# Order of VectorE, GpSimd and ScalarE work around the seven-product gate and up matmuls of a two-block transformer kernel

## The chip, the cores and the metric

One core of a Trainium2 chip runs the whole program. The metric is the device time of one execution in microseconds (us). TensorE is PE in the profile (its weight loads PEld), VectorE is DVE, ScalarE is ACT, GpSimd is POOL, and SyncE (SP) issues the DMAs.

## What is computed

Two blocks of two layers each work on 512 tokens of width 1024. Every one of the four layers ends in a gated feed-forward part with 2816 hidden columns, and the change lies in that part alone:

```python
def rms_norm(x, g):
    xf = x.astype(jnp.float32)
    y = xf * lax.rsqrt(jnp.mean(xf * xf, axis=-1, keepdims=True) + EPS)
    return (y * g.astype(jnp.float32)).astype(x.dtype)

# first block, both layers
    h = rms_norm(x, g_ffn_pre)
    gate, up = jnp.split(jnp.matmul(h, w_gate_up), [FFN_HIDDEN], axis=-1)
    f = jnp.matmul(jax.nn.silu(gate) * up, w_down)
    return x + rms_norm(f, g_ffn_post)

# second block, both layers
def swiglu(xn, w_gate, w_up, w_down):
    return (jax.nn.silu(xn @ w_gate) * (xn @ w_up)) @ w_down
        h = h + swiglu(rmsnorm(h, norm_ffn[l]), ffn_w_gate[l], ffn_w_up[l], ffn_w_down[l])
```

Ahead of it stand retention, dilated attention and a spatial gate (first block), or sparse attention or a convolution and cross attention (second block). They are as they were.

## The kernel before

All values are float32. A product of two float32 matrices is made of three TensorE passes (`mm3`, L384 to L387): each operand is held as a high half (ScalarE casts it to the rounded type, "cast") and a low half (VectorE subtracts the high half from the source, "low"), and high times high, high times low and low times high are summed in a PSUM bank.

`ffn` (L565) is called once for each of the four layers. The normalised input lies turned in `xh` and `xl` (8 blocks of 128 x 512 tokens). The four token blocks reach it one after the other: `settle` (L436) adds a block's result into `x`, `sq` squares it on ScalarE (L425), `sc` scales it on VectorE (L430), `transposer` (L401) turns it on TensorE (L407), casts it (L395) and takes the low part (L396). In the first block (`post` is true) `settle` also scales the two PSUM banks on VectorE (L457) and adds them (L461). The first two hidden blocks of 128 (`prod`, L580) are computed as plain products, for tokens 0 to 255 first, while blocks 2 and 3 of the tokens still arrive.

The other 20 hidden blocks go in 20 **units**: a unit is a pair of weight tiles, gate for two hidden blocks (even units) or up for the same two (odd units). `seven` (L666) computes a unit's 2 x 2 product of halves with seven half-size products instead of eight, 12 matmuls of 256 columns each. For that a unit's weights are prepared on the way: `unit` (L257) has the steps `cast1`/`low1` (tile a, slot s1), `t13` (two GpSimd subtractions in place of tile b and a, L283 and L284; the first overwrites a's first half, so it must come after `low1`), `cast4`/`low4` (half of b), `t24` (two VectorE subtractions, L287 and L288, which need `t13` and `low4` done), `cast2`/`low2` and `cast3`/`low3`. The low parts are all L270, the casts L266. On the other side the products are combined: ScalarE copies the first (L700, `m1`), VectorE adds (L705, L714, L718, L723, L724), the last sum of a unit is `whole_sum` (L684), followed for gate units by the silu on ScalarE (L686), and after an up unit `gated` multiplies up into gate (L690).

The order is written by hand: after product r of unit i the function s_r of unit i queues its share of both kinds of work (L694 to L726), so that VectorE's queue holds, unit after unit, L287, L288, L718, low2, L723, L724, low3, L684, low1, (L690 after an up unit,) L705, low4, L714. The products' sums of the input (`act` s1 to s4) are made once, from four whole copies of input quarters: two by `whole` (L629) on GpSimd, two copied by ScalarE out of the transposes' banks (L417), combined on VectorE (`mix`, L633) and split (L640, L644).

PSUM has eight banks b0 to b7. In `seven` the third product takes bank 2 in even units and bank 7 in odd ones. The down product (`down`) follows, in all eight banks: block t of the tokens takes banks 2t and 2t+1. Its weights are split by `pump` (casts L249, lows L250), its inputs by `hsplit` (cast L395, low L396 into `sh`). `_Clock` (L165) only orders the recording; the engines run by semaphores.

Of the kernel before, what the change touches and what calls it, by code (L numbers as in the profile page):

```python
# [199 lines left out]
class _Weights:  # L200
# [53 lines left out]
            if not moved:  # L254
                return

    def unit(self):  # L257

        V, S, G = self.nc.vector, self.nc.scalar, self.nc.gpsimd
        u = {}  # L260
# [19 lines left out]
        def t13():  # L280
            b = u["b"] = self.r.pop(u["j"])
            u["b12"], u["b22"] = (b[:, 512 * i:512 * i + 512] for i in range(2))
            G.tensor_sub(u["b11"], u["b12"], u["b11"])  # L283
            G.tensor_sub(u["b12"], u["b12"], u["b22"])  # L284

        def t24():
            V.tensor_sub(u["b22"], u["b22"], u["b11"])  # L287
# [35 lines left out]
def tile_mixers(ctx: ExitStack, tc: tile.TileContext, a: dict, widths: list, out: bass.AP):  # L323
# [48 lines left out]
    def bank(i):  # L372
        return psum.tile([P, T], F32, tag=f"b{i}", name=f"b{i}")
# [25 lines left out]
    def transposer(xn, t, dst, banks):  # L399
        dh, dl = dst  # L400

        def go(halves=(0, 1)):
            for half in halves:
                b = bank(banks[half])
                for kk in range(4):
                    k = 4 * half + kk
                    PE.transpose(b[:, kk * P:(kk + 1) * P], xn[:, k * P:(k + 1) * P], ident)  # L407
                ks = slice(4 * half, 4 * half + 4)
                if dl is None:
                    S.copy(dh[:, ks, cols(t)], blocks(b))  # L410
                else:
                    split_from(dh[:, ks, cols(t)], dl[:, ks, cols(t)], blocks(b))
                    if keep["x"] is not None and dh is xh and t > 1:
                        kept.append((keep["x"][half][:, :, (t - 2) * P:(t - 1) * P], blocks(b)))
                        keep["t"].add(t)
            while kept:
                S.copy(*kept.pop(0))  # L417
        return go

    turned = {}  # L420
# [144 lines left out]
    def ffn(pend, post, nxt, last=False):  # L565
# [82 lines left out]

        def unit(i):
            if i not in ops:  # L650
                ops[i] = W.unit()
            return ops[i]

        def prep(i, *names):
# [13 lines left out]
        def seven(i):  # L668


            n, j = units[i]
            b1, b2, b3, b6, b7, b45 = (bank(k) for k in (0, 1, 2 + 5 * (i % 2), 3, 4, 5 + i % 2))
            p1, p2, p3, p6, p7 = (z[:, :256] for z in (b1, b2, b3, b6, b7))
            p4, p5 = b45[:, :256], b45[:, 256:]
            m1, u2, u3, u4 = (st["pc"][:, 256 * k:256 * k + 256] for k in range(4))
# [16 lines left out]
            last = done[-2] if i else (lambda: None,) * 2  # L692

            def s0():  # L694
                last[0]()
                W.done(int(i > 0))
                prep(i + 1, "low1")

            def s1():
                S.copy(m1, p1)  # L700
                prep(i + 1, "t13")
                last[1]()

            def s2():
# [24 lines left out]
            for r, (p, f) in enumerate(zip(todo, (s0, s1, s2, s3, s4, s5, s6))):  # L729
                product(i, *p)  # L730
                f()
                if i == 0 and r == 0:
                    sum_low("s1", 3)()
                if i == len(units) - 1:
                    if r == 5:
                        hsplit(0)
                    W.pump(1)
                W.prefetch()
                yield

# [12 lines left out]
        late = len(steps) - 4  # L753
        keep.update(x=(quarter(full(0)), quarter(full(3))), t=set())

        def fill(t):
            if t not in keep["t"] and turned[t]:
                for half in range(2):
# [3 lines left out]

        def unit0(*names):
            return lambda: prep(0, *names)
        also(0, whole(1, 0, 0, G), unit0("cast1"))
        also(1, whole(2, 4, 0, G), unit0("low1"))
        also(2, lambda: fill(2))
        also(late - 1, lambda: fill(2), lambda: fill(3), lambda: keep.update(x=None), unit0("t13", "cast4"), mix(3, 0, 3, 1), mix(4, 3, 1, 0), mix(2, 2, 4, 0),
             sum_high("s2", 4), sum_high("s4", 2))
        also(late, unit0("low4"), sum_low("s4", 2), unit0("t24", "cast2"), sum_low("s2", 4))  # L770
        also(late + 1, unit0("low2"), mix(0, 0, 1, 0), sum_high("s3", 0))
# [8 lines left out]
            g = seven(i)  # L780
            steps += [(12 * 0.119, lambda g=g: next(g))] * 7
        steps.append((0, last_sums))
        steps.append((0, lambda: (two(0), nxt(), hsplit(1))))

        TAIL = 4
        acc = {}
# [1197 lines left out]
```

## Time and profile before

| | |
|---|---|
| median of 3 runs | 2797.47 us (2794.26 to 2797.48) |
| the profiled execution | 2799.59 us, of which the profiled span is 2797.8 us |
| PE busy | 2677.8 us, 96% of the span, 16568 matmuls |
| DVE busy | 1809.4 us, 65% |
| ACT busy | 1182.2 us, 42% |
| POOL busy | 782.4 us, 28% |
| chain that ended last, by engine | PE 51%, DVE 23%, POOL 12%, ACT 10%, issue 4% |

The first four engine rows are busy time; a busy PE is not a PE at its peak, since matmuls are pipelined. The last row follows the work that ended last backwards from the final instruction, each step to what released it. Rows further down have the start in us from the span's start, the duration in us, engine, line, operation, written and read tiles with shapes, and in brackets the engine's idle time before the instruction and what ended it.

### The profile page before, as it was taken

What the parts mean: (1) busy time and instruction counts of PE and PEld (TensorE: products, weight loads), DVE (VectorE), ACT (ScalarE), POOL (GpSimd) and SP (SyncE); (2) the same over time, 40 slices, a digit from 0 to 9 for tenths busy, and PEclk for the clock granted to TensorE, in tenths of its full rate; (3) what the DMA queues carried; (4) which work ended last, traced back from release to release, by engine and by line L of the source; (5) the groups of instructions that cost most, each with busy time, mean ns of one, the idle gap of its engine ahead of it and who ended that gap; (6) DMA issues with size and microseconds to landing.
All of it is one profiled execution on the core that took longest, in us unless ns stands there. A gap on an engine that the chain in (4) does not pass through costs nothing.

```text
span 2797.8 us, 41468 instructions
## 1 busy us (share of the span) xinstructions
PE 2677.8 (96%) x16568; PEld 2378.7 (85%) x16568; DVE 1809.4 (65%) x2733; ACT 1182.2 (42%) x2015; POOL 782.4 (28%) x662
## 2 busy tenths in 40 slices
PE   8999999999999999999999999999998889999999
PEld 7888999889788999878677889998886578899987
DVE  4555888545565888453985437887379744488852
ACT  3434444333434444333444434444256544344431
POOL 3231333002232232012451312331049913133300
PEclk9999999999999999999999999999999999999999
DMA  4221232323121323423232212333232312133331
GB/s 154 78 68 67 91 106 98 130 75 108 61 80 53 102 98 101 138 70 102 64 124 83 91 38 91 106 103 124 91 119 91 113 30 92 46 91 106 99 116 65
DMA packets 76225, 256.42 MB, mean 92 GB/s; under 512 B 10368, under 2 KB 11776, under 8 KB 76032
## 3 DMA queue, kind: packets, MB, share of 16 engines
q1 hardware_dynamic: 76032, 253.77, 28.3%
q8 instruction: 130, 2.13, 0.3%
q14 instruction: 63, 0.52, 0.1%
HBM read 251.64 MB, written 2.10 MB: 91 GB/s over the span
## 4 chain that ended last, share of the span: by engine, by line
PE 51%; DVE 23%; POOL 12%; ACT 10%; issue 4%; DMA 1%; POOLq 0%; ACTq 0%; DVEq 0%; SPq 0%
PE b L385 15%; PE b L387 15%; PE b L386 14%; DVE hl L270 8%; ACT hl L266 5%; POOL raw L283 5%; POOL raw L284 4%; DVE raw L287 2%; DVE hl L250 2%; DVE b L1759 2%; DVE hraw L684 2%; ACT hl L249 1%; PE b L407 1%; PE b L1639 1%; DVE xn L430 1%
## 5 line engine op out<-in xcount | busy, mean ns | idle before, releaser
L385 PE MATMUL b<-xh,hl 128*128 128x256 f32 (+1 forms) x1728 | 505.5, 293 | 4.0 <-DVE xn L457 2.4
L386 PE MATMUL b<-xl,hl 128*128 128x256 f32 (+1 forms) x1728 | 504.1, 292 | 1.7 <-DVE xl L396 1.7
L387 PE MATMUL b<-xh,hl 128*128 128x256 f32 (+1 forms) x1728 | 503.6, 291 | 0.0
L266 ACT CAST hl<-raw 128x1024 fp32r<-128x1024 f32 x320 | 286.7, 941 | 391.1 <-DVE raw L287 391.1
L385 PE MATMUL b<-hl,xh 128*128 128x512 f32 (+2 forms) x1152 | 439.1, 381 | 4.9 <-ACT xh L395 3.1
L386 PE MATMUL b<-hl,xh 128*128 128x512 f32 (+2 forms) x1152 | 422.6, 367 | 1.7 <-DVE hl L250 1.7
L387 PE MATMUL b<-hl,xl 128*128 128x512 f32 (+2 forms) x1152 | 423.0, 367 | 0.2
L270 DVE TENSOR_TENSOR hl<-raw,hl 128x1024 fp32r<-128x1024 f32 x320 | 387.1, 1210 | 9.4 <-ACT hl L266 1.3
L250 DVE TENSOR_TENSOR hl<-raw,hl 128x1024 fp32r<-128x1024 f32 (+2 forms) x249 | 303.4, 1232 | 137.8 <-ACT hl L249 135.7
L249 ACT CAST hl<-raw 128x1024 fp32r<-128x1024 f32 (+2 forms) x308 | 303.5, 1000 | 101.9 <-PE b L387 60.1
L385 PEld LDWEIGHTS b<-xh,hl 128*128 128x128 f32 x1728 | 331.4, 192 | 11.4 <-issue 3.4
L386 PEld LDWEIGHTS b<-xl,hl 128*128 128x128 f32 x1728 | 331.3, 192 | 7.8 <-DVE xl L396 2.7
L387 PEld LDWEIGHTS b<-xh,hl 128*128 128x128 f32 x1728 | 331.2, 192 | 5.4
L283 POOL TENSOR_TENSOR raw<-raw 128x512 f32<-128x512 f32 x80 | 140.2, 1752 | 567.3 <-DVE hl L270 502.7
L387 PE MATMUL b<-hl,sh 128*128 128x512 f32 x704 | 276.3, 392 | 7.2 <-DVE sh L396 7.2
L385 PE MATMUL b<-hl,sh 128*128 128x512 f32 x704 | 276.7, 393 | 2.2 <-ACT sh L395 2.2
L387 PE MATMUL b<-sh,hl 128*128 128x256 f32 x960 | 270.8, 282 | 5.8 <-DVE hl L270 5.8
L386 PE MATMUL b<-hl,sh 128*128 128x512 f32 x704 | 276.0, 392 | 0.0
L385 PE MATMUL b<-sh,hl 128*128 128x256 f32 x960 | 269.2, 280 | 1.1 <-ACT hraw L576 1.1
L386 PE MATMUL b<-sh,hl 128*128 128x256 f32 x960 | 267.9, 279 | 0.0
L385 PEld LDWEIGHTS b<-hl,xh 128*128 128x128 f32 x1152 | 219.3, 190 | 35.1 <-issue 7.0
L386 PEld LDWEIGHTS b<-hl,xh 128*128 128x128 f32 x1152 | 219.4, 190 | 25.9 <-DVE hl L250 3.0
(304 smaller groups left out, 4745.2 us busy)
## 6 DMA issues: line engine op xcount, KB each, us to landing
raw<-in_ws SPq DMA_DIRECT2D x400, 512.0 KB, 3.6
raw<-in_ws SPq DMA_DIRECT2D x64, 384.0 KB, 3.1
x<-in_x SPq DMA_DIRECT2D x4, 512.0 KB, 6.6
mem<-in_mem SPq DMA_DIRECT2D x4, 512.0 KB, 5.6
out<-x SPq DMA_DIRECT2D x4, 512.0 KB, 2.6
raw<-in_ws SPq DMA_DIRECT2D x4, 336.0 KB, 2.8
gain<-in_g_mix_pre SPq DMA_DIRECT2D x2, 512.0 KB, 4.7
gain<-in_g_mix_post SPq DMA_DIRECT2D x2, 512.0 KB, 4.4
```

Source lines behind the costliest of these rows:

```text
L249: self.nc.scalar.copy(t[:, 0, :w], r[:, :w])
L250: self.low.tensor_sub(t[:, 1, :w], r[:, :w], t[:, 0, :w].bitcast(F32))
L266: S.copy(u[name][:, 0, :n], src())
L270: return lambda: V.tensor_sub(u[name][:, 1, :n], src(), u[name][:, 0, :n].bitcast(F32))
L283: G.tensor_sub(u["b11"], u["b12"], u["b11"])
L284: G.tensor_sub(u["b12"], u["b12"], u["b22"])
L287: V.tensor_sub(u["b22"], u["b22"], u["b11"])
L385: PE.matmul(o, lh, rh, start=first, stop=False)
L386: PE.matmul(o, lh, rl, start=False, stop=False)
L387: PE.matmul(o, ll, rh, start=False, stop=last)
L684: V.tensor_add(c[:, :, 256:], u3[:, None, :].to_broadcast([P, 2, 256]), halves(b45))
L1759: V.scalar_tensor_tensor(acc[g], i, w, acc[g], op0=OP.mult, op1=OP.add)
```

## The change

Five things change, all in `ffn` and what it calls.

- In a unit's first step, the next unit's `low1` and `t13` are queued ahead of the finished unit's `whole_sum`; they stood behind it.
- For the first unit of each `ffn` the two subtractions of `t13`, and for each `ffn` the two `whole` sums, run on VectorE instead of GpSimd.
- ScalarE's copies of turned input (`kept`) are no longer queued right behind their transposes but by `flush`, two steps of the plan later, behind casts of weights.
- The third product's bank is swapped: 7 in even units, 2 in odd ones.
- In the last unit, weight tiles of the down product are split after four of the seven products instead of all, and the first two hidden blocks are split after products 4 and 5 (the first was after product 5, the second behind the last sum).

```diff
-    def unit(self):
+    def unit(self, first=False):
...
-            G.tensor_sub(u["b11"], u["b12"], u["b11"])
-            G.tensor_sub(u["b12"], u["b12"], u["b22"])
+            e = V if first else G
+            e.tensor_sub(u["b11"], u["b12"], u["b11"])
+            e.tensor_sub(u["b12"], u["b12"], u["b22"])
...
-            while kept:
-                S.copy(*kept.pop(0))
...
-                ops[i] = W.unit()
+                ops[i] = W.unit(not i)
...
-            b1, b2, b3, b6, b7, b45 = (bank(k) for k in (0, 1, 2 + 5 * (i % 2), 3, 4, 5 + i % 2))
+            b1, b2, b3, b6, b7, b45 = (bank(k) for k in (0, 1, 7 - 5 * (i % 2), 3, 4, 5 + i % 2))
...
             def s0():
+                prep(i + 1, "low1", "t13")
                 last[0]()
                 W.done(int(i > 0))
-                prep(i + 1, "low1")
 
             def s1():
                 S.copy(m1, p1)
-                prep(i + 1, "t13")
                 last[1]()
...
                 if i == len(units) - 1:
-                    if r == 5:
-                        hsplit(0)
-                    W.pump(1)
+                    if r in (0, 2, 4, 6):
+                        W.pump(1)
+                    if r in (4, 5):
+                        hsplit(r - 4)
...
+        def flush():
+            while kept:
+                S.copy(*kept.pop(0))
...
-        also(0, whole(1, 0, 0, G), unit0("cast1"))
-        also(1, whole(2, 4, 0, G), unit0("low1"))
-        also(2, lambda: fill(2))
-        also(late - 1, lambda: fill(2), lambda: fill(3), ...
+        us, g = steps[0]
+        steps[0] = (us, lambda g=g: (whole(1, 0, 0, V)(), g()))
+        also(0, whole(2, 4, 0, V), unit0("cast1"))
+        also(1, unit0("low1"))
+        also(2, flush, lambda: fill(2))
+        also(late - 1, flush, lambda: fill(2), lambda: fill(3), ...
...
-        steps.append((0, lambda: (two(0), nxt(), hsplit(1))))
+        steps.append((0, lambda: (two(0), nxt())))
```

What it moves in VectorE's queue, at three places. Lines of the kernel after are one to three off those before (L683 is `whole_sum`, L689 `gated`, L703 was L705, L712 was L714, L288 was L287). First, in the middle of the units of the first layer, around an up unit's last sum (b_2993). Before:

```order
L270 TENSOR_TENSOR hl<-raw,hl 128x1024
L684 TENSOR_TENSOR hraw<-pc,b_2993 128x2x256
L270 TENSOR_TENSOR hl<-raw,hl 128x1024
L690 TENSOR_TENSOR hraw<-hraw 128x1024
L705 TENSOR_TENSOR hraw<-pc,b_3107 128x256
L270 TENSOR_TENSOR hl<-raw,hl 128x512
```

After:

```order
L270 TENSOR_TENSOR hl<-raw,hl 128x1024 x2
L683 TENSOR_TENSOR hraw<-pc,b_2993 128x2x256
L689 TENSOR_TENSOR hraw<-hraw 128x1024
L703 TENSOR_TENSOR hraw<-pc,b_3107 128x256
L270 TENSOR_TENSOR hl<-raw,hl 128x512
```

`low1` (the second L270) now stands directly behind `low3` and ahead of the sum and of `gated`. Second, VectorE at the start of the first layer's `ffn`, from the transposes of token block 2 (banks b_2337, b_2344) to those of block 3 (b_2474, b_2481). Before:

```order
L396 TENSOR_TENSOR xl<-b_2344,xh 128x4x128
L250 TENSOR_TENSOR hl<-raw,hl 128x1024
L457 SCALAR_TENSOR_TENSOR xn<-b_2253,sm,gain 128x512
L457 SCALAR_TENSOR_TENSOR xn<-b_2254,sm,gain 128x512
L461 TENSOR_TENSOR x<-x,xn 128x1024
...
L396 TENSOR_TENSOR xl<-b_2481,xh 128x4x128
L633 TENSOR_TENSOR hraw<-hraw 128x1024 x3
```

After:

```order
L397 TENSOR_TENSOR xl<-b_2344,xh 128x4x128
L628 TENSOR_TENSOR hraw<-xh,xl 128x1024
L250 TENSOR_TENSOR hl<-raw,hl 128x1024
L628 TENSOR_TENSOR hraw<-xh,xl 128x1024
L456 SCALAR_TENSOR_TENSOR xn<-b_2253,sm,gain 128x512
...
L397 TENSOR_TENSOR xl<-b_2481,xh 128x4x128
L284 TENSOR_TENSOR raw<-raw 128x512
L285 TENSOR_TENSOR raw<-raw 128x512
L632 TENSOR_TENSOR hraw<-hraw 128x1024 x3
```

The two `whole` sums (L628) and the first unit's `t13` (L284, L285) are new in this queue. Third, VectorE in the last unit of the first layer, where L705, L714 and L724 read banks 1, 3 and 7. Before:

```order
L250 TENSOR_TENSOR hl_4909<-raw_4752,hl_4909 128x1024
L705 TENSOR_TENSOR up_4876<-pc_2628,b1_4871 128x256
L714 TENSOR_TENSOR pc_2628<-pc_2628,b3_4873 128x256
L718 TENSOR_TENSOR pc_2628<-pc_2628,b4_4874 128x256
L396 TENSOR_TENSOR sh_4965<-hraw_2336,sh_4965 128x512
L723 TENSOR_TENSOR pc_2628<-pc_2628,b6_4875 128x256
L724 TENSOR_TENSOR up_4876<-pc_2628,b7_4872 128x256
L684 TENSOR_TENSOR up_4876<-pc_2628,b6_4875 128x2x256
L690 TENSOR_TENSOR hraw_2336<-hraw_2336,up_4876 128x1024
L396 TENSOR_TENSOR sh_4988<-hraw_2336,sh_4988 128x512
```

After:

```order
L703 TENSOR_TENSOR up_4876<-pc_2628,b1_4871 128x256
L250 TENSOR_TENSOR hl_4922<-raw_4752,hl_4922 128x1024
L712 TENSOR_TENSOR pc_2628<-pc_2628,b3_4873 128x256
L397 TENSOR_TENSOR sh_4952<-hraw_2336,sh_4952 128x512
L716 TENSOR_TENSOR pc_2628<-pc_2628,b4_4874 128x256
L397 TENSOR_TENSOR sh_4968<-hraw_2336,sh_4968 128x512
L721 TENSOR_TENSOR pc_2628<-pc_2628,b6_4875 128x256
L722 TENSOR_TENSOR up_4876<-pc_2628,b2_4872 128x256
L683 TENSOR_TENSOR up_4876<-pc_2628,b6_4875 128x2x256
```

The splits of the first two hidden blocks (`sh`) stand earlier, and L722 reads bank 2 where L724 read bank 7. ScalarE's queue here has the same kinds of instructions in the same order as before; the orders of TensorE and of the DMAs have not moved.

## Rows read from the trace of the kernel before

**Rows 1.** Waits of PE, whole run: waiter, releaser, us in total, times, longest.

```profile
PE b L387 <- DVE hl L270: 5.8, 24, 0.3
PE b L385 <- DVE xn L457: 2.4, 2, 1.2
PE b L387 <- DVE sh L396: 7.2, 4, 1.8
```

**Rows 2.** Waits of PE from 268 to 502 us, the first layer's gate and up.

```profile
PE b L407 <- DVE xn L430: 0.9, 2, 0.5
```

**Rows 3.** Timeline of PE: third product of two even units, one pair apart.

```profile
331.19 0.28 PE L385 MATMUL b<-sh,hl 128*128 128x256 f32 x1
...
351.21 0.28 PE L385 MATMUL b<-sh,hl 128*128 128x256 f32 x1
```

**Rows 4.** Timeline of DVE over two units, first layer.

```profile
472.27 0.69 DVE L287 TENSOR_TENSOR raw<-raw 128x512 f32<-128x512 f32 x1 [0.86 <-POOL raw L284]
...
477.15 0.68 DVE L684 TENSOR_TENSOR hraw<-pc,b 128x512 f32<-128x512 f32 x1
477.74 1.22 DVE L270 TENSOR_TENSOR hl<-raw,hl 128x1024 fp32r<-128x1024 f32 x1
479.21 0.42 DVE L705 TENSOR_TENSOR hraw<-pc,b 128x256 f32<-128x256 f32 x1 [0.25 <-ACT pc L700]
479.73 1.15 DVE L270 TENSOR_TENSOR hl<-raw,hl 128x512 fp32r<-128x512 f32 x1
...
482.07 0.69 DVE L287 TENSOR_TENSOR raw<-raw 128x512 f32<-128x512 f32 x1 [0.85 <-POOL raw L284]
...
487.54 1.22 DVE L270 TENSOR_TENSOR hl<-raw,hl 128x1024 fp32r<-128x1024 f32 x1
488.68 1.22 DVE L690 TENSOR_TENSOR hraw<-hraw 128x1024 f32<-128x1024 f32 x1
490.03 0.42 DVE L705 TENSOR_TENSOR hraw<-pc,b 128x256 f32<-128x256 f32 x1
490.37 1.23 DVE L270 TENSOR_TENSOR hl<-raw,hl 128x512 fp32r<-128x512 f32 x1
...
492.78 0.69 DVE L287 TENSOR_TENSOR raw<-raw 128x512 f32<-128x512 f32 x1 [0.86 <-POOL raw L284]
```

**Rows 5.** Timeline of POOL over the same two units.

```profile
479.04 1.30 POOL L283 TENSOR_TENSOR raw<-raw 128x512 f32<-128x512 f32 x1 [6.80 <-DVE hl L270]
...
488.84 2.21 POOL L283 TENSOR_TENSOR raw<-raw 128x512 f32<-128x512 f32 x1 [6.81 <-DVE hl L270]
491.12 1.62 POOL L284 TENSOR_TENSOR raw<-raw 128x512 f32<-128x512 f32 x1
```

**Rows 6.** Timeline of ACT behind a gate unit's last sum.

```profile
477.86 1.06 ACT L686 ACTIVATE hraw<-hraw 128x1024 f32<-128x1024 f32 x1 [1.92 <-DVE hraw L684]
478.82 0.35 ACT L700 COPY pc<-b 128x256 f32<-128x256 f32 x1
```

**Rows 7.** Timeline of DVE at the start of the first layer's gate and up.

```profile
281.72 2.31 DVE L430 SCALAR_TENSOR_TENSOR xn<-x,sm,gain 128x1024 f32<-128x1024 f32 x1 [0.77 <-POOL sm L392]
...
287.45 1.23 DVE L633 TENSOR_TENSOR hraw<-hraw 128x1024 f32<-128x1024 f32 x1 [0.65 <-ACT hraw L417]
```

**Rows 8.** Timeline of POOL at the same place.

```profile
281.65 1.30 POOL L283 TENSOR_TENSOR raw<-raw 128x512 f32<-128x512 f32 x1
283.02 2.13 POOL L284 TENSOR_TENSOR raw<-raw 128x512 f32<-128x512 f32 x1
```

**Rows 9.** Timeline of DVE at the start of the first layer's down product.

```profile
503.95 0.68 DVE L396 TENSOR_TENSOR sh<-hraw,sh 128x512 fp32r<-128x512 f32 x1
...
505.00 0.42 DVE L724 TENSOR_TENSOR up<-pc,b 128x256 f32<-128x256 f32 x1
```

**Rows 10.** Timeline of PE at the same place.

```profile
504.69 0.50 PE L387 MATMUL b<-hl,sh 128*128 128x512 f32 x1 [1.80 <-DVE sh L396]
```

**Rows 11.** Busy times by stretch, PEclk (share of 2.4 GHz) third from the end.

```profile
505.25:508.60 3.35, 3.35 (x9) 2.59 (x8) 3.31 (x6) 2.31 (x4) 0.00 (x0) 0.51 0.71 251
```

More of the change, by code (lines that the diff above doesn't have):

```diff
@@ L764, in unit0 @@
             return lambda: prep(0, *names)
-        also(0, whole(1, 0, 0, G), unit0("cast1"))
-        also(1, whole(2, 4, 0, G), unit0("low1"))
-        also(2, lambda: fill(2))
-        also(late - 1, lambda: fill(2), lambda: fill(3), lambda: keep.update(x=None), unit0("t13", "cast4"), mix(3, 0, 3, 1), mix(4, 3, 1, 0), mix(2, 2, 4, 0),
+        us, g = steps[0]
[3 more added lines that the diff above has]
+        also(2, flush, lambda: fill(2))
+        also(late - 1, flush, lambda: fill(2), lambda: fill(3), lambda: keep.update(x=None), unit0("t13", "cast4"), mix(3, 0, 3, 1), mix(4, 3, 1, 0), mix(2, 2, 4, 0),
              sum_high("s2", 4), sum_high("s4", 2))
```

## The prediction
> **What bounds the kernel now.** TensorE is busy 96% of the span, so only its waits can be won. I read in this order: what PE waits for, PE's own pace where it doesn't wait, and then the queues of the engines it waits for.
>
> PE's waits that end in the lines touched here are four kinds [rows 1, 2]: 24 waits for a low part (L270), 7.2 us for the first split hidden block at the start of the four down products (L396), 2 x 1.2 us for L457, and 0.9 us for L430. They look small, but what they stand for is larger. Where PE doesn't wait, the third product of two even units lies 351.21 - 331.19 = 20.02 us apart [rows 3], 168 matmuls of 0.119 us. VectorE's queue needs 492.78 - 472.27 = 20.51 us for the same two units [rows 4], and stands waiting for GpSimd's L284 before L287 in both, 0.86 and 0.85 us. So VectorE and GpSimd are slower than PE by 0.49 us in each pair of units. PE starts the stage some way ahead of them in what it has ready: of nine pairs in a layer only the last six show a wait (24 in four layers), so the reserve is about 9 x 0.49 - 6 x 0.49 = 1.5 us. At the end of a stage it is gone, and **the end of each gate and up stage is set by the VectorE chain, not by PE**. That chain runs low1, then GpSimd's t13 (L283, L284), then L287, L288, low2, low3, L684 and low1 again.
>
> How the two engines meet is in the same rows. L283 takes 1.30 us when it comes first (479.04), and low4, 128 x 512 elements, then takes 1.15 instead of L287's 0.69: it ends 0.54 us after L283 does. Behind L690, which started at 488.68 and ends at 489.90, L283 takes 2.21 and ends 1.15 us after L690 [rows 4, 5]. L705, whose second input lies in PSUM, takes its 0.42 us beside L283 and neither is lengthened. So instructions with both inputs in SBUF exclude each other on the two engines, for their whole length, whoever comes first. At the stage's start it goes the other way round: L283 at 281.65 first, L430 held to 2.31 us, and L284 held to 2.13 behind L430, although L430 had been waiting when L283 ended [rows 7, 8].
>
> The Trainium skill, "SBUF — State Buffer", section "Who interferes with whom", states this as a rule: a VectorE instruction with two SBUF inputs and a GpSimd instruction that reads SBUF take one shared interface, and the one issued first blocks the other fully. The trace agrees. It speaks against the change in one place: low1 earlier lets L283 go ahead of L690, so L690 is now the one that is blocked. By the rule an up unit comes to the 10.55 us worked out below, without it to some 9.7, which is the first rival.
>
> **The units.** Nothing is added; low1 moves ahead of L684, and t13 behind low1 with it. I lay out both units from the start of L287 (0).
>
> Behind a gate unit (L287 at 472.27) L684 starts now at 4.88 and low1 ends at 6.69. After: low1 4.88 to 6.10, L684 6.02 to 6.70. GpSimd starts 0.08 behind low1: L283 6.18 to 7.48, L284 7.56 to 8.85, if nothing holds it. But the silu (L686) waits for L684, ScalarE's copy L700 stands behind the silu, and L705 waits for the copy [rows 4, 6]: silu 6.73, copy 7.69 to 8.04, L705 8.07, low4 0.52 later at 8.59. There it is held by L284 to 8.85 and ends 0.54 later, 9.39; L714 0.4 more, next L287 at 9.70. Before it was 9.80 (482.07). So of the 0.60 us by which low1 is earlier only 0.1 is left: low1 used to fill the time of the silu, and now VectorE idles there 1.4 us.
>
> Behind an up unit (L287 at 482.07): low1 ends at 6.10, L283 6.18 to 7.48. L690 wants to start at 6.74, is held to 7.48 and needs 1.07 more: 8.55. L284, held by L690, ends 1.13 later at 9.68. L705 0.13 behind L690, 8.68; low4 is held to 9.68, ends 10.22; L714 from 10.14, L287 at 10.55. Before it was 10.71. The port's pieces are the same (L283, L690, L284, low4), only in another order, so 0.16 is won and not 0.60.
>
> A pair becomes 9.70 + 10.55 = **20.25 us instead of 20.51**, still above PE's 20.02. Nine pairs: 9 x 0.26 = 2.3 us a layer earlier at the end of the chain. PE's waits fall from 2.9 us to 9 x 0.23 - 1.5 = 0.6 a layer.
>
> **The start.** The `whole` sums on VectorE are two more instructions of 1.22 us (the size of L690) in front of L457, but the low part that stood there held by GpSimd's sums no longer is; and t13 on GpSimd no longer holds L430 (1.2 instead of 2.31). I take the 1.2 us for L457 and 0.5 for L430 as won in the two layers of the first block: 1.7 us. In the second block there is no L457, and L430 isn't waited for. Against it, the first unit's t13 now costs VectorE 2 x 0.69 = 1.38 us ahead of L633; 0.65 of it falls into a wait that L633 has now for ScalarE's copies [rows 7], 0.7 stays on the chain. Together -1.0 in each of two layers, +0.7 in each of the other two: **-0.6 in all**. Bounds: if the 0.65 doesn't cover, +1.3 more in four layers; if the 0.7 meets the reserve, -2.8. The bank swap takes away one PE wait at the third product of the first unit (0.3 us), but the chain then lags PE there and takes it back: nothing. The copies behind the casts: ScalarE has nothing waiting at that place, nothing.
>
> **The end.** In the last unit the order of casts stays; on VectorE the first split L396 comes ahead of L718 and behind only one L250 that had to wait, by my addition 0.6 us earlier than at 503.95 + 0.68 now [rows 9]. But L724 now reads bank 2, which the down product wants six matmuls after its first, and the second split stands ahead of it: L724 would end at about 505.76 instead of 505.42. PE, which waits for the split until 504.69 [rows 10], reaches that bank four matmuls later (4 x 0.24), at 505.73; after, 505.82 at equal lag. So +0.1 a layer, **+0.4 in all**; the 0.6 is paid back at the bank.
>
> **The clock.** In the first layer the granted clock is 0.51 just after this gap [rows 11], the 1.2 GHz level, for 3.35 us, at a cost of about 3.35 x 0.49 = 1.6 us; the same follows in three of the four layers. PE's idle time there becomes shorter and is cut in three pieces (0.7, 1.2 and 0.7 us instead of 0.7 and 1.8). Whether the clock still falls no row tells: from none (-5) to all four (+1.6). I take two, **-1.6**.
>
> **Sum.** 4 x -2.3 = -9.2, -0.6, +0.4, -1.6: -11.0 us. The profiled execution took 2799.59, 2.1 above the median; the same difference from the median of 2797.47 gives **2786.5 us**.
>
> **Rivals.**
> *PE's own pace.* If L690 isn't held behind L283 (the rows show low4 and L430 held, L690 never in second place), its unit takes some 9.7 too, the pair drops under 20.02, and PE bounds the stage. Chain: 9 x 0.49 = 4.4 a layer, PE's waits gone, clock never falling: 4 x -4.4 - 0.6 + 0.4 - 5 = -23, 2774.5. The ending of low4 after L283 speaks against it. Chance 0.14.
> *Little changes.* The up unit's gain of 0.16 comes from a difference of order alone, and the gate unit's 0.10 from a ScalarE chain whose gaps I took from another order. If both vanish, the pair stays at 20.4 to 20.5: 4 x -0.5 - 0.2, and the clock as now: 2795. The split of the wait would then only have moved from L287 to L690 and L705. Chance 0.18.
> *Slower.* When L283 ends, L690 and L284 both want the port. If L284, 0.08 us behind, gets it, L690 ends 1.3 us later: L284 7.56 to 8.85, L690 to 9.92, L705 10.05, low4 10.4 to 11.1, L287 at 11.4. Pair 21.1, 9 x 0.6 = 5.4 a layer: 4 x 5.4 - 0.2 = +21, 2819. It turns to a loss when the pair passes 20.52. L430 at 281.72, which went ahead of L284, is the evidence against. Chance 0.08.
> My forecast has the other 0.60, with 2781 to 2791 of its own (0.1 us a pair is 3.6 us; one fall of the clock 1.6).
>
> **Numbers.** Within 0.2% (5.6 us, about what a measurement of this kernel can tell from no change) begins at 2791.9. Faster: 0.57 of the forecast, all 0.14, 0.05 of the little change: 0.76. Slower 0.08, the same 0.16. The range for 8 in 10 leaves out the slower case and half of each of the other two: 2776 to 2794.5.
>
> **What would show it.** In the trace after: L287 9.7 and 10.55 us apart by turns; L690 at 1.7 to 1.8 us instead of 1.22, starting ahead of L284; 0.9 us of wait at L287 gone and 1.4 us of idle time before L705 behind the silu instead; the first PE wait for low2 (L270) not before the sixth pair; no PE wait for L457; at the down product two PE waits of VectorE, for L396 and for the bank of L724. It is wrong if the pairs stand at 20.02 (then PE bounds), or if L284 starts ahead of L690.

## The result, and the profile after

The changed kernel takes 2785.31 us (median of 7 runs, 2774.03 to 2788.40) against 2799.28 us for the kernel before in the same sessions (7 runs, 2794.26 to 2804.07). The ratio is 0.9942, with a 95% interval of 0.9924 to 0.9961: 14 us less by the medians, 16 by the ratio. The forecast was 2786.5 us. The profiled execution took 2781.26 us, with a span of 2779.3 us.

Some more line numbers of after, called so from here on: t13 is L284 and L285, the silu L685, ScalarE's copy L699, the sum that frees the third product's bank L722, the split of a hidden block L396 (high part) and L397 (low part), and low1 to low4 are L270 in both kernels.

First VectorE's queue, the two units that [rows 4] show, from one L288 to the next but one (columns: start us, duration, engine, line, operation, out<-in, size, and in brackets the idle time before it and what ended it).

```profile
466.65 0.68 DVE L288 TENSOR_TENSOR raw<-raw 128x512 f32<-128x512 f32 x1
...
470.38 2.35 DVE L270 TENSOR_TENSOR hl<-raw,hl 128x1024 fp32r<-128x1024 f32 x2
472.65 0.68 DVE L683 TENSOR_TENSOR hraw<-pc,b 128x512 f32<-128x512 f32 x1
474.71 0.42 DVE L703 TENSOR_TENSOR hraw<-pc,b 128x256 f32<-128x256 f32 x1 [1.38 <-ACT pc L699]
475.24 0.78 DVE L270 TENSOR_TENSOR hl<-raw,hl 128x512 fp32r<-128x512 f32 x1
...
476.28 0.68 DVE L288 TENSOR_TENSOR raw<-raw 128x512 f32<-128x512 f32 x1
...
482.27 0.68 DVE L683 TENSOR_TENSOR hraw<-pc,b 128x512 f32<-128x512 f32 x1
482.99 1.82 DVE L689 TENSOR_TENSOR hraw<-hraw 128x1024 f32<-128x1024 f32 x1
...
485.27 1.23 DVE L270 TENSOR_TENSOR hl<-raw,hl 128x512 fp32r<-128x512 f32 x1
...
486.75 0.68 DVE L288 TENSOR_TENSOR raw<-raw 128x512 f32<-128x512 f32 x1
```

GpSimd in the same stretch, the rows that answer [rows 5]:

```profile
472.81 1.29 POOL L284 TENSOR_TENSOR raw<-raw 128x512 f32<-128x512 f32 x1 [6.96 <-DVE hl L270]
474.18 1.30 POOL L285 TENSOR_TENSOR raw<-raw 128x512 f32<-128x512 f32 x1
482.43 1.29 POOL L284 TENSOR_TENSOR raw<-raw 128x512 f32<-128x512 f32 x1 [6.96 <-DVE hl L270]
483.80 2.15 POOL L285 TENSOR_TENSOR raw<-raw 128x512 f32<-128x512 f32 x1
```

Behind the gate unit the next L288 comes after 476.28 - 466.65 = 9.63 us, behind the up unit after 486.75 - 476.28 = 10.47. Over the pairs of all four layers the two are 9.62 to 9.66 and 10.47 to 10.50: **20.12 us a pair instead of 20.51**. Both new waits are where they were expected. Behind the gate unit VectorE stands idle for 1.38 us until the copy behind the silu is there. Behind the up unit L284 goes first and L689 pays, 1.82 us instead of the 1.22 that it took ahead of the change; L285 then takes 2.15 behind L689, and low4 1.23 behind L285.

TensorE's waits in the lines of this stage, over the whole run, which answer [rows 1]:

```profile
PE b L388 <- DVE sh L397: 4.8, 4, 1.2
PE b L387 <- DVE xl L643: 2.5, 4, 0.6
PE b L386 <- DVE up L722: 2.1, 4, 0.5
```

The 24 waits for low2 and the two for the scaled block (L457) are gone. The wait for the low part of the first split hidden block went from 7.2 to 4.8 us. The wait for its high part, which the rows ahead of the prediction leave out, is nearly gone too: before, it was this row, and in after 0.09 to 0.17 us are left of each.

```profile
PE b L385 <- ACT sh L395: 2.2, 4, 0.6
```

Two waits are new: s1's low part (L643) in the first unit, and the bank of the up sum (L722) at the start of the down product. This is that start, the place of [rows 10], and the clock in the 28 us from there on in each layer (columns of the second view as in [rows 11]):

```profile
496.12 0.50 PE L386 MATMUL b<-hl,sh 128*128 128x512 f32 x1
...
498.04 0.50 PE L388 MATMUL b<-hl,sh 128*128 128x512 f32 x1 [1.19 <-DVE sh L397]
...
499.76 0.50 PE L386 MATMUL b<-hl,sh 128*128 128x512 f32 x1 [0.52 <-DVE up L722]
```

```profile
496.00:524.00 28.00, 26.17 (x113) 21.06 (x114) 20.70 (x26) 14.00 (x19) 0.00 (x0) 1.00 0.61 207
...
2652.90:2680.90 28.00, 26.28 (x113) 21.17 (x114) 20.54 (x26) 13.88 (x18) 0.00 (x0) 1.00 0.54 169
```

The rows of the first and the last layer; in the two between, the granted clock is 1.00 as well, its 2.4 GHz level; before, it fell for 3.4 us in three of the four.

**A ruler for the experiments.** One run's time moves by more than most of these edits are worth (after: 2774 to 2788). So each kernel is read at the same matmuls of TensorE: from the first product of the first unit to the third product of the second and of the last unit, to the first matmul of the down product and to its 121st. In the first layer of after the ends of this ruler are:

```profile
294.70 0.28 PE L386 MATMUL b<-xh,hl 128*128 128x256 f32 x1
...
525.73 0.39 PE L386 MATMUL b<-hl,sh 128*128 128x512 f32 x1
```

that is 231.03 us; the four layers of one run agree to 0.1 us where the clock doesn't fall, and a fall of the clock at the start of the down product adds 1.6 (before: 233.85 without one, 235.45, 235.44 and 235.39 with one), or 0.9 to 1.0 where it hides the wait for the bank ("after, old order" and "after, s1 first"). The table gives a layer without a fall; the last two columns are the falls at the four down products in the one profiled run of each kernel, and the time (median with its ratio to before, or the one run's). A ratio is taken against before in the same session (2799.1 to 2802.4 us), so the times of two rows aren't to be set against each other to a few us.

| kernel | second unit | last unit | down, first | down, 121st | falls | time, us |
|---|---|---|---|---|---|---|
| before | 13.45 | 196.11 | 204.45 | 233.85 | 3 | 2799.3 |
| order alone | 13.43 | 193.55 | 200.92 | 230.33 | 3 | 2786.5, 0.9951 [0.9936, 0.9966] |
| after | 13.87 | 193.99 | 201.42 | 231.03 | 0 | 2785.3, 0.9942 [0.9924, 0.9961] |
| after, old order | 13.86 | 196.55 | 204.89 | 234.53 | 2 | 2798.6, 0.9992 [0.9981, 1.0004] |
| after, start on GpSimd | 13.35 | 193.47 | 200.85 | 230.47 | 1 | 2778.0 (one) |
| after, old banks | 13.95 | 194.07 | 201.40 | 230.22 | 0 | 2777.5 (one) |
| after, copies ahead of casts | 13.87 | 193.99 | 201.40 | 231.03 | 2 | 2793.0 (one) |
| after, s1 first | 13.02 | 193.28 | 201.23 | 230.85 | 3 | 2783.9 (one) |
| before, late silu | 13.43 | 195.99 | 203.63 | 231.55 | 0 | 2785.9, 0.9950 [0.9930, 0.9969] |
| after, late silu | 13.87 | 193.99 | 201.12 | 228.35 | 0 | 2775.0 (one) |
| three edits | 13.00 | 193.12 | 200.25 | 227.47 | 0 | 2768.4, 0.9885 [0.9868, 0.9901] |
| three edits, start on GpSimd | 12.89 | 193.01 | 200.13 | 227.36 | 0 | 2765.9, 0.9870 [0.9856, 0.9885] |

### The profile page after: what moved, and what is told of

Same layout as the page of the kernel before. It is cut to its first block, busy times and chain, and to the rows that moved or that the text cites. A ratio compares the mean times of both kernels' runs of the same rounds, so it can differ in the third digit from the quotient of the medians.

```text
span 2779.3 us, 41456 instructions
## 1 busy us (share of the span) xinstructions
PE 2667.3 (96%) x16568; PEld 2374.0 (85%) x16568; DVE 1821.3 (66%) x2749; ACT 1180.9 (42%) x2015; POOL 724.2 (26%) x646
## 4 chain that ended last, share of the span: by engine, by line
PE 66%; DVE 19%; ACT 7%; issue 4%; POOL 2%; DMA 0%; DVEq 0%; ACTq 0%; POOLq 0%
PE b L386 20%; PE b L388 19%; PE b L387 19%; DVE hl L270 5%; ACT hl L266 3%; DVE hl L250 2%; DVE b L1764 1%; DVE hraw L689 1%; PE b L408 1%; PE b L1644 1%; ACT hl L249 1%; DVE raw L288 1%; DVE hraw L683 1%; DVE xn L429 1%; DVE mask L1422 1%
## 5 line engine op out<-in xcount | busy, mean ns | idle before, releaser
L250 DVE TENSOR_TENSOR hl<-raw,hl 128x1024 fp32r<-128x1024 f32 (+2 forms) x249 | 298.0, 1210 | 135.0 <-ACT hl L249 133.0
L270 DVE TENSOR_TENSOR hl<-raw,hl 128x1024 fp32r<-128x1024 f32 x320 | 368.1, 1169 | 9.4 <-ACT hl L266 1.3
L249 ACT CAST hl<-raw 128x1024 fp32r<-128x1024 f32 (+2 forms) x308 | 303.2, 1000 | 102.6 <-PE b L388 60.1
L284 POOL TENSOR_TENSOR raw<-raw 128x512 f32<-128x512 f32 x76 | 102.0, 1342 | 593.5 <-DVE hl L270 587.3
L387 PEld LDWEIGHTS b<-hl,xh 128*128 128x128 f32 x1152 | 219.3, 190 | 26.2 <-DVE hl L250 3.4
```

The source lines that it names most:

```text
L249: self.nc.scalar.copy(t[:, 0, :w], r[:, :w])
L250: self.low.tensor_sub(t[:, 1, :w], r[:, :w], t[:, 0, :w].bitcast(F32))
L270: return lambda: V.tensor_sub(u[name][:, 1, :n], src(), u[name][:, 0, :n].bitcast(F32))
L284: e.tensor_sub(u["b11"], u["b12"], u["b11"])
L387: PE.matmul(o, lh, rl, start=False, stop=False)
```

## The experiments

**1. The order alone, in before.**

```diff
 def s0():
+    prep(i + 1, "low1", "t13")
     last[0]()
     W.done(int(i > 0))
-    prep(i + 1, "low1")
 def s1():
     S.copy(m1, p1)
-    prep(i + 1, "t13")
     last[1]()
```

> Before, with one edit: the next unit's low1 and t13 come ahead of the finished unit's sum; all else as before. Theory (the order alone gives the gain of the units): VectorE's two first lines of a pair lie 9.63 + 10.49 = 20.12 us apart instead of 9.80 + 10.71 = 20.51; the third products lie 10.01 apart in every unit after the first, none 10.50 apart; TensorE's 24 waits for low2 are gone, 3.0 us a layer; the start keeps its waits (2 x 1.2 for L457, 0.9 for L430) and its first interval of 10.10. The time is about 12 us below that of before, and more if the clock falls less often. Rival (the sums on VectorE and the bank swap at the start carry the gain): the pairs stay at 20.4 or more, and the time within 4 us of before.

VectorE's L287 come 9.63 and 10.49 us apart by turns, the third products 10.01 in every unit after the first. In the first layer TensorE waits here:

```profile
PE b L387 <- DVE sh L396: 1.8, 1, 1.8
PE b L385 <- DVE xn L457: 1.2, 1, 1.2
PE b L407 <- DVE xn L430: 0.9, 2, 0.5
```

No wait for low2 is left, and these three stand as before; the wait of 0.55 us for the split's high part is down to 0.06 to 0.26. The stage is 3.5 us shorter (233.85 to 230.33), four times that is 14.1 us, and the time is 13.6 us lower. The theory holds: this one edit carries the change. The clock falls in three of four layers as before, and the gain is there all the same, so it isn't the clock's.

**2. Everything but the order.** The same edit undone in after.

> After, with one edit undone: low1 again behind the finished unit's sum and t13 behind that. Theory: pairs back at 20.51 us (9.80 and 10.71), six intervals of 10.50 in each layer, the down product some 3 us a layer later than in after; time 2795 to 2799. Rival (the gain is the clock's at the start of the down product, or the start's): pairs may go back, but the time stays within 4 us of after, 2782 to 2789.

The pairs are back at 9.80 + 10.71, and in the first layer TensorE waits for low2 six times again (five intervals of 10.50 and one of 10.12, where six of 10.50 were expected):

```profile
PE b L388 <- DVE hl L270: 1.4, 6, 0.2
PE b L388 <- DVE sh L397: 1.2, 1, 1.2
```

The stage takes 234.53 us, and the time isn't to be told from before (0.9992). So the other edits together give nothing that the times can show.

**3. The start on GpSimd.**

```diff
-                ops[i] = W.unit(not i)
+                ops[i] = W.unit()
...
-        us, g = steps[0]
-        steps[0] = (us, lambda g=g: (whole(1, 0, 0, V)(), g()))
-        also(0, whole(2, 4, 0, V), unit0("cast1"))
-        also(1, unit0("low1"))
+        also(0, whole(1, 0, 0, G), unit0("cast1"))
+        also(1, whole(2, 4, 0, G), unit0("low1"))
```

> After, with the start of the stage undone: the whole sums and the first unit's t13 on GpSimd again. Theory: the 2 x 1.2 us for L457 come back in layers 1 and 2 and 0.7 with L430; and the interval from the first to the second unit's third product goes from 10.99 back to 10.10 in all four layers, because the two first differences (2 x 0.69 us) no longer stand on VectorE ahead of what makes s1's low part. Against after the down product then starts about +1.0 in layers 1 and 2, -0.9 in layers 3 and 4. Rival (s1's low part is late because low1 and t13 of the second unit now come ahead, with GpSimd's differences in the way): the interval stays at 10.99 and TensorE's wait for L643 at 0.6.

Two misses. The wait of 1.2 us for the scaled block did not come back: TensorE turns token block 2 at 26.49 us ahead of the first unit's first product, against 26.21 in after and 28.05 before. And the first interval went to 10.47, not to 10.10. What did come back is a wait of 0.34 us ahead of the turning of block 3; first this run, then after, up to the down product:

```profile
PE b L408 <- DVE xn L429: 0.7, 2, 0.4
```

```profile
PE b L408 <- DVE xn L429: 0.4, 1, 0.4
```

L429 is held there by GpSimd's first difference (2.30 us instead of 1.28). So the 0.28 us between this kernel and after are what the first differences on VectorE give; with the copies out of the way, the sums on VectorE give nothing that shows. VectorE in the first layer, first in before, then here:

```profile
273.92 2.98 DVE L250 TENSOR_TENSOR hl<-raw,hl 128x1024 fp32r<-128x1024 f32 x1 [1.60 <-ACT hl L249]
```

```profile
271.11 1.29 DVE L397 TENSOR_TENSOR xl<-b,xh 128x512 fp32r<-128x512 f32 x2 [1.48 <-ACT xh L396]
272.55 2.10 DVE L250 TENSOR_TENSOR hl<-raw,hl 128x1024 fp32r<-128x1024 f32 x1
274.57 1.40 DVE L456 SCALAR_TENSOR_TENSOR xn<-b,sm,gain 128x512 f32<-128x512 f32 x2
```

L250 is still held by GpSimd's sums, 2.10 instead of 1.22. But it begins right behind the split, where before it began behind a wait of 1.60 us for ScalarE's cast L249. That cast no longer has the copies ahead of it. In the units, the first differences on VectorE cost 0.52 us (13.87 to 13.35, and as much in the second block's two layers, where block 2 is turned at the same place in both kernels), which comes through to the end of the stage (231.03 to 230.47). So moving the start to VectorE wins 0.28 us in two layers and loses some 0.5 in four.

**4. The copies ahead of the casts again, the sums still on VectorE.**

```diff
                         keep["t"].add(t)
+            while kept:
+                S.copy(*kept.pop(0))
         return go
```

> After, with one edit undone: ScalarE's copies for the whole sums stand again right behind the casts of the transposed block, ahead of the casts that others wait for. From the run with the start undone (transposes of the first unit's block 26.49 us ahead of the first product, against 26.21 in after and 28.05 before) the copies' place alone gives 1.56 of the 1.84 us. Theory now: the copies hold the cast behind which low1's neighbour L250 waits, and either edit is enough for the 1.2 us of L457: with the sums on VectorE the cast ends by 272.4, when VectorE comes free, so this kernel stands at 26.2 to 26.5. Rival (the copies' place is the only cause): back at 28.0 and TensorE's wait of 2 x 1.2 us for the scaled block is back.

```profile
272.51 1.21 DVE L630 TENSOR_TENSOR hraw<-xh,xl 128x1024 f32<-128x1024 f32 x1
274.19 1.23 DVE L250 TENSOR_TENSOR hl<-raw,hl 128x1024 fp32r<-128x1024 f32 x1 [0.47 <-ACT hl L249]
...
276.47 1.40 DVE L458 SCALAR_TENSOR_TENSOR xn<-b,sm,gain 128x512 f32<-128x512 f32 x2
```

```profile
PE b L386 <- DVE xn L458: 0.6, 1, 0.6
```

In between: 26.77 us, 0.56 more than after and outside the expected 26.2 to 26.5, and TensorE's wait for the scaled block is back at half its size (0.58 us in each of the two layers); the one ahead of block 3 (L431 in this kernel) is not. L250 waits 0.47 for the cast even here. So the copies' place takes the whole wait of 1.21 us for the scaled block away by itself (experiment 3), and the sums on VectorE by themselves 0.63 of it: for that wait the two edits cover each other. The same run shows the chance in the clock: its down product starts with the same two waits as in after, and the clock falls in two layers, where in after it fell in none.

**5. The banks as before.** `2 + 5 * (i % 2)` again for the third product's bank, in after.

> After, with the banks of the third product as before (2 in the first unit and 7 in the last). Theory: at the start of the stage the wait of 0.45 us at the first unit's third product is back, but the second unit's third product is then no later than in after, since it waits for VectorE's s1 low part anyway; at the down product the 0.5 us wait for the up sum (L722) is gone, so that the down product's tenth matmul starts 0.5 earlier. Net about -0.5 a layer, -2 us: the bank swap gives nothing here. Rival: the 0.45 comes through to the end, and the swap earns 0.45 a layer at the start.

```profile
PE b L388 <- DVE sh L397: 1.2, 1, 1.2
PE b L386 <- ACT hraw L575: 0.8, 1, 0.8
```

The first unit waits 0.8 us for its bank (more than the 0.45 expected), and the second unit's third product is only 0.08 later than in after. At the down product the bank wait is gone. The stage is 0.8 us shorter: 230.22. The bank swap of the change thus costs 0.8 us a layer; what it takes away was hidden.

**6. The silu later on ScalarE.**

```diff
             def whole_sum():
                 V.tensor_add(c[:, :, 256:], u3[:, None, :].to_broadcast([P, 2, 256]), halves(b45))
+
+            def silu():
                 if not j:
                     S.activation(c, c, AF.Silu)
...
-            done.append((whole_sum, gated))
-            last = done[-2] if i else (lambda: None,) * 2
+            done.append((whole_sum, gated, silu))
+            last = done[-2] if i else (lambda: None,) * 3
...
                 prep(i + 1, "cast4")
+                last[2]()
                 W.done()
```

> After, with one edit: the gate unit's silu is issued to ScalarE behind the next product's copy and behind the cast of low4, instead of ahead of both. Theory (the silu holds the gate unit through ScalarE's copy, as the prediction had it): VectorE's 1.4 us of idle time ahead of L703 goes, and the gate unit falls from 9.63 to 9.2 us. Rival (the gate unit is held by the pieces that exclude each other behind low1: 2 x 1.3 on GpSimd and low4's 0.7 in any order): low4 now goes between GpSimd's two differences and holds the second for 0.7, the next first line waits for it, and the gate unit stays at 9.55 to 9.65. Either way TensorE's third products stay 10.01 apart. At the start of the down product the 2.06 us in which VectorE waits for the first down tile's cast behind the silu goes, and TensorE's wait for the first split hidden block (1.2 us in each layer) with it, at least in part: down to 0.2 to 0.6.

VectorE and then GpSimd behind a gate unit (some line numbers are two or three higher here):

```profile
467.56 0.68 DVE L683 TENSOR_TENSOR hraw<-pc,b 128x512 f32<-128x512 f32 x1
468.15 0.41 DVE L705 TENSOR_TENSOR hraw<-pc,b 128x256 f32<-128x256 f32 x1
468.49 1.08 DVE L270 TENSOR_TENSOR hl<-raw,hl 128x512 fp32r<-128x512 f32 x1
...
470.74 0.69 DVE L288 TENSOR_TENSOR raw<-raw 128x512 f32<-128x512 f32 x1 [0.62 <-POOL raw L285]
```

```profile
467.71 1.30 POOL L284 TENSOR_TENSOR raw<-raw 128x512 f32<-128x512 f32 x1 [6.96 <-DVE hl L270]
469.09 1.62 POOL L285 TENSOR_TENSOR raw<-raw 128x512 f32<-128x512 f32 x1
```

The gate unit takes 9.19 us. The theory's 9.2 holds, and so does half of the rival's picture: low4 does go between the two differences, and L288 does wait for L285. But low4 holds L285 for 0.3 us only, because L284, low4 and L285 now follow each other with nothing between them. A pair takes 9.19 + 10.50 = 19.69 us, less than TensorE's 20.02, and in the last two pairs of each layer VectorE waits for TensorE (the up unit takes 10.82 there). At the down product no wait is left:

```profile
493.82 0.40 PE L386 MATMUL b<-hl,sh 128*128 128x512 f32 x1
...
494.29 0.39 PE L388 MATMUL b<-hl,sh 128*128 128x512 f32 x1
```

The down product's third matmul is 0.47 us behind its first, where it was 1.92 in after. The stage is 2.7 us shorter, 228.35 or 228.36 in every layer. Most of this is not won in the units: behind the last gate unit, ScalarE's cast of the first down tile (L249) stood behind the silu, and VectorE waited for it. That wait of 2.06 us stands in after and, as long, in before; here it is gone:

```profile
494.36 1.23 DVE L250 TENSOR_TENSOR hl<-raw,hl 128x1024 fp32r<-128x1024 f32 x1 [2.06 <-ACT hl L249]
```

```profile
500.40 2.44 DVE L250 TENSOR_TENSOR hl<-raw,hl 128x1024 fp32r<-128x1024 f32 x2 [2.06 <-ACT hl L249]
```

**7. The late silu in before.** The same edit, low1 and t13 as they were.

> Before, with one edit: the gate unit's silu behind the next product's copy and the cast of low4, the order of low1 and t13 as before. Theory (the silu costs only where low1 doesn't fill its time): the gate unit stays within 0.1 of 9.80 and the pair above 20.3, so TensorE's waits for low2 remain, 20 or more of them; but at the start of the down product the first down tile's cast no longer stands behind the silu and the wait of 1.8 us shrinks by 1 or more, and the clock then falls there less often. Time 2787 to 2793. Rival (the silu holds the pair in before too): pair 20.1 or less, no waits for low2, 2776 to 2783, and low1's place wasn't needed.

```profile
PE b L387 <- DVE hl L270: 5.6, 24, 0.2
PE b L387 <- DVE sh L396: 1.5, 4, 0.4
```

The pair stays at 9.79 + 10.71, the 24 waits stay, and the wait at the down product falls from 7.2 to 1.5 us. As the theory has it: with low1 behind the sum, the silu's time was filled, and only the end gains. The wait for the high part is gone too. That is still 2.3 us a layer and the clock's falls, 13 us in the time (about 1 us below the expected range), nearly as much as the change itself gives. So of the 2.7 us of experiment 6 only some 0.4 come from the units, if the end gains alike in both kernels.

**8. s1's low part first.**

```diff
 def s0():
+    if i == 0:
+        sum_low("s1", 3)()
     prep(i + 1, "low1", "t13")
 ...
-                if i == 0 and r == 0:
-                    sum_low("s1", 3)()
```

> After, with one edit: in the first unit the low part of s1 comes ahead of the second unit's low1 and first differences. Theory (TensorE's 0.6 us wait for L643 in each layer is VectorE's low1 of 1.2 us standing ahead): that wait is gone and the first interval goes from 10.99 to 10.1 or less, 0.9 us a layer at the second unit. Whether it reaches the end: if the stage's end is set by TensorE now, the down product starts 0.9 earlier in each layer; rival: the VectorE chain is no earlier, so TensorE's wait for the first split hidden block grows from 1.2 to 2.1 and the end stays.

The second unit comes 0.85 us earlier, and the wait for L643 is gone. At the last unit 0.7 of it is left, since TensorE waits a little for VectorE again (0.10 in two of the last units), and at the down product:

```profile
497.52 0.50 PE L386 MATMUL b<-hl,sh 128*128 128x512 f32 x1 [0.55 <-ACT sh L396]
...
499.45 0.57 PE L388 MATMUL b<-hl,sh 128*128 128x512 f32 x1 [1.19 <-DVE sh L397]
```

The wait for the split's high part is back at what it was before the change, and the down product is at most 0.2 us earlier. The rival holds, in another row than it named: in after, the VectorE and ScalarE chain still sets the end of the stage, and an earlier TensorE only waits longer.

**9 and 10. Together.** The late silu, s1's low part first, and the first unit's third product in bank 6 with the old banks for the others; then the same with the start on GpSimd.

> After, with three edits: the late silu, s1's low part first, and the third product of the first unit in bank 6, of the others as before the change (so that the down product waits for no bank). If each reaches the end: from the first unit's first product to the 27th matmul of the down product 209.7 less 0.9 (s1), 0.8 (bank) and 0.6 to 1.0 (silu): 207.0 to 207.4 in each layer; time 2785.3 - 4 x 2.4 = 2776. Rival (the VectorE chain sets the end and its parts don't add up): 208.9 as in the kernel with the bank swap undone; 2782.

> As the last kernel, but with the start of the stage undone (whole sums and the first unit's differences on GpSimd). From the run with the start undone in after: 0.3 us later at the first unit in layers 1 and 2, and 0.5 earlier at the second unit in all four, if s1's low part still holds the first unit. If s1's low part ahead of low1 already frees that, TensorE has no use for the 0.5, and this kernel is 0.3 us later in layers 1 and 2 and equal in 3 and 4: no difference that the times can show, within 3 us of the last kernel.

The stages take 227.47 and 227.36 us, and the times are 2768.4 and 2765.9 us, 1.2% and 1.3% below before. In both, the view of TensorE's waits from the first layer's first unit to some 25 us into its down product is empty. That is more than expected: 206.2 and 206.1 us to the 27th matmul of the down product instead of 207.0 to 207.4, since the silu's part is 2.7 us and not 0.6 to 1.0. s1's low part first, worth at most 0.2 us in experiment 8, gives 0.9 us a layer here: the second unit is 0.87 earlier than in experiment 6, and the end 0.88, since the chain no longer sets the end. The bank's 0.8 give nothing more, since the late silu alone had ended that wait (no run has the bank or s1's part alone with the late silu). The two kernels can't be told apart, as expected.

## Why the prediction was right, step by step

**The units** were right in mechanism and in each event. From the start of L288, behind the gate unit: L703 at 8.06 (forecast 8.07), low4 at 8.59 (8.59), its end at 9.37 (9.39). Behind the up unit: L689 ends at 8.53 (8.55), L285 at 9.67 (9.68), low4 at 10.22 (10.22). What was mis-sized is the last step, from the end of low4 to the next L288: 0.31 and 0.33 in the forecast, 0.26 and 0.25 in the trace. That is 0.13 us a pair, so 20.12 instead of 20.25, and nine pairs make 3.5 us a layer instead of 2.3: **-14.1 us instead of -9.2**, which experiment 1 gives by itself. It also made TensorE's waits for low2 vanish, where 0.6 us a layer was forecast to be left: nine pairs at 0.10 above TensorE's 20.02 make 0.9 us, less than the reserve.

The Trainium skill, "SBUF — State Buffer", section "Who interferes with whom", has issue order decide which of the two engines blocks the other, and the blocked one wait in full. L689 behind L284 agrees: it ends 1.09 us after L284 does, and takes 0.60 us longer than its own 1.22. The first rival, that L690 isn't held, is refuted by the row 482.99, and the slower one, that L285 goes ahead of L689, by 483.80 and its 2.15 us.

**The start** was right in sign, small in size, and wrong in half of its cause. Forecast -1.0 us in each of two layers and +0.7 in the other two, -0.6 in all. The transposes are 1.84 us earlier (forecast 1.7), and against the order alone the last unit is 0.44 later: -1.4, -1.4, +0.4 and +0.4, **-1.9 in all**. The 0.5 us for L430 came as forecast, by the first differences leaving GpSimd: that wait was 0.49 before, 0.34 in experiment 3, and is gone in after and in experiment 4. The step that failed is the 1.2 us for L457, put down to the sums on VectorE, while "the copies behind the casts" were costed at nothing because ScalarE had nothing waiting there. Experiments 3 and 4 show that the copies' place alone takes the whole wait away, and that VectorE's sums add nothing to it; alone they take half (1.21 to 0.58). The cast L249 stood behind the copies, and L250 waited 1.60 us for it; that wait is one line in the trace of before, and it ends on the engine that was said to be free. The first differences on VectorE cost 0.52 (forecast 0.7).

**The end** was right in mechanism (two waits, the second for the bank of the up sum) and somewhat small: with the order in both, the path from the last unit's third product to the 121st matmul takes 230.33 - 193.55 = 36.78 us in the order alone and 231.03 - 193.99 = 37.04 in after, so +0.26 a layer and **+1.0 in all** instead of +0.4. Both of its terms are seen in experiment 5: without the swap the path is 230.22 - 194.07 = 36.15 us, 0.63 less than in the order alone, as the 0.6 of the forecast has it for the earlier split; the swap then takes 0.89 back, where 0.7 was forecast. Of the three pieces of TensorE's idle time that the prediction gives (0.7, 1.2 and 0.7 us) the first is 0.09 to 0.17 and the third 0.52; the second is 1.19.

**The clock** was forecast at -1.6, two falls instead of three. In the profiled run there was none, -4.8. The kernels with after's start of the down product have no fall, one and two (after, experiments 3 and 4), three of twelve places, so two of four was within what occurs and the profiled run was at the good end.

**The sum** of these in the profiled run is -14.1 - 1.9 + 1.0 - 4.8 = -19.8 us, with +1.3 outside this stage, so that the span is 18.5 us shorter. The medians differ by 14.0. The forecast of -11.0 is nearer to the medians than to this run, in which the clock never fell at these four places. The mean granted clock is 0.992 for the fastest run of after (2774.03), 0.990 for the profiled one and 0.987 to 0.989 for the five slower ones; 0.003 of 2780 us is some 8 us (an estimate), about as far as they lie apart, so most of this spread is the clock's, but only the profiled run has a trace, and where it fell in the others stays open. The middle of the forecast is thus partly luck: the units gave 4.9 us more than forecast, and the medians show no gain beyond the units. The sign and the carrier are not luck (experiments 1 and 2).

**"1.4 us of idle time before L705"** was the best hint in the prediction, and it wasn't followed: it was booked as the price of the new order. What makes it is a ScalarE queue that can be reordered, and that is worth 2.7 us a layer (experiment 6), where the whole change gives 233.85 - 231.03 = 2.8 by the same ruler. But the price wasn't in the units, where the prediction saw it: the same silu made VectorE wait 2.06 us at the end of the stage, before the change and after it, and taking that away is 2.3 of the 2.7 (experiment 7). The prediction's account of the end has no term for it.

**Two sums** in the prediction are off and change nothing: 0.65 us in each of four layers is 2.6, not 1.3; and 4 x 0.24 behind 504.69 is 505.65, where 505.73 needs the 0.33 that the first of these four steps takes (504.69 to 505.02 in the trace of before).

## What to carry to other kernels

When an edit moves work off a wait, look at what stands at the waiter's place afterwards: a new idle time with one instruction behind it in another engine's queue is the next edit. Then look for the same instruction at the ends of the stage, where an idle time reaches TensorE in full: here the silu's place was worth some 0.4 us a layer in the units and 2.3 at the end. Before costing a moved instruction at nothing, list what stands behind it on its own engine and who waits for that, not only what the engine itself waits for. And an edit on an engine that doesn't set the end yet (s1's low part) can be worth nothing today and its full price once the bound has moved, so it is tried again after each change of the bound.

## What the runs showed of the hardware

When a VectorE instruction with both inputs in SBUF has begun beside one of GpSimd's differences and is held by it, VectorE goes next, ahead of the GpSimd instruction that follows 0.08 us later: low4 in experiment 6 (waiting from 468.49, L284 done at 469.01, L285 then taking 1.62 instead of 1.30), L689 in after, and [rows 7, 8] of before. No pair of L284 and L285 in these traces shows it the other way.

The clock does not fall by the length of TensorE's wait alone. At the start of the down product, with a wait of 1.80 us, it fell in three of four layers each in before (behind a wait of 0.55) and in the order alone (behind 0.06 to 0.26); with 1.19 and 0.52 us in none, one and two of four (after, experiments 3 and 4); with 0.56 ahead of 1.19 in two and three of four (experiments 2 and 8); with 1.19 alone in none of four (experiment 5). Where that start has no wait or one of 0.4 us (experiments 6, 7, 9 and 10), it fell in none of sixteen. The order alone in its first two layers (the other two read 0.94 too):

```profile
497.20:525.20 28.00, 26.13 (x108) 21.18 (x108) 19.47 (x26) 13.59 (x19) 0.00 (x0) 0.94 0.61 207
1107.00:1135.00 28.00, 26.21 (x115) 21.37 (x116) 21.07 (x27) 13.80 (x18) 0.00 (x0) 1.00 0.65 208
...
```

0.94 over 28 us is a fall to 1.2 GHz for 3.4 us, and costs 1.6 us. What decides between layers with equal waits stays open.
